# Mixers of a two-layer decoder: splitting the q and k projections by pairs of heads, and the order around it

## The chip, the cores and the metric

One core of one Trainium2 chip runs the whole program in one launch. The metric is the time on the device in microseconds (us), the median of the runs. An execution's time is a little longer than its span in the profile, which goes from the first to the last instruction.

The engines are named as in the profile: PE is TensorE (matmuls; PEld are its weight loads), DVE is VectorE, ACT is ScalarE, POOL is GpSimd, and SP is SyncE, which issues nearly all transfers here. L650 is line 650 of the kernel before.

## What is computed

Two layers on 528 positions (16 meta tokens and 512 of the input) of 1024 features. Each has a mixer and a gated feed-forward part with a short convolution. The mixer is where the change lies:

```python
def mixer_sublayer(h, ...):
    u = rms_norm(h, pre_g)
    z = jnp.einsum("bld,de->ble", u, w_in)
    q, k, v, f_logit, a_val, a_gate, sc_b, sc_c, sc_x = jnp.split(z, idx, axis=-1)
    log_f = jax.nn.log_sigmoid((f_logit + b_forget).astype(jnp.float32))
    y_attn = forgetting_attention(q, k, v, log_f)       # 8 heads of 64
    a = causal_depthwise_conv(a_val * jax.nn.sigmoid(a_gate), a_dw_w) + a_dw_b    # 31 taps
    a = jax.nn.silu(layer_norm(a, a_ln_g, a_ln_b))
    y_conv = jnp.einsum("blc,ce->ble", a, a_pw_w)
    y_sc = sc_b * causal_depthwise_conv(sc_c * sc_x, sc_conv_w)                   # 3 taps
    y = jnp.concatenate([y_attn, y_conv, y_sc], axis=-1)
    y = jnp.einsum("ble,ed->bld", head_rms_norm(y, head_g), w_out)
    return h + rms_norm(y, post_g)

# attention: logit[t,s] = q_t.k_s / 8 + F[t] - F[s] for s <= t, F = inclusive cumsum of log_f
```

## The kernel before

**Layout and arithmetic.** Features lie on the 128 partitions and positions along the free axis, in two halves of 264. Every large product is made of three fp32r matmuls: each operand x is split into a high part (x rounded to fp32r, written by ACT) and a low part (x minus its high part, written by DVE), and high times high, low times high and high times low are added in PSUM. `mm3` at L650 issues these, so L650 stands for all projections, for w_out and for the feed-forward products. Weights come by transfer into `raw`, are split by ACT (`whi`, L619 in planned stretches) and DVE (`wlo`, L623) into rotating buffers, three of the normal kind and five wide ones.

**The order.** In a mixer and in the products that follow it (`finish`), an event simulation at build time (class `Flow`) decides the order of the instructions on each engine. Every operation is given to it with an engine, a planned duration, the tokens it waits for, a priority (a lower number goes first) and a latency; generators called threads stand for PE's work. The resulting order of each engine is fixed in the program. At run time an engine waits only for semaphores, in that order. `flow.run(flow.settled)` ends a planned stretch when what is left has priority 2 or more, which is the default of weight loads and splits (`plan_block`).

**A mixer.** `fill` runs the projections in the order of `mixer_steps()`: q and k blocks hold two heads each (q j and k j are heads 2j and 2j+1), v blocks four heads; sc_b, sc_c and sc_x belong to the short convolution; "pw" starts `conv_tail`, the layer norm, SiLU and pointwise product of the 31-tap convolution. The taps themselves (L966, 60 instructions a layer) are DVE's filler with priority 4. Side by side with `fill` run:

- `maxima`: for each head, PE makes the logits from the high parts of q and k alone (L1372), DVE takes each row's maximum (L1379), POOL puts the negated maxima on a diagonal (L1387), a matmul with ones turns them into a row (L1396), and ACT copies the row into a spare partition of the q tile (L1398). A head's maxima start when the head before has begun its logits.
- `exponentials`: `logits` (two matmuls, L1416: the second one brings the products with the low parts), ACT's exponential (L1423) into tile `pf`, POOL's clearing of the causal corner (L1430), and `weigh` (L1450), the product with v into one accumulator bank (`acc`, a single bank). Each head has two query ranges, 0 to 128 and 128 to 528. After each, ACT evacuates the bank twice, Square into `sq` (L1463) and copy into `yta` (L1464); both must be done before the bank is used again.
- `att_norms`: for each pair of heads a matmul over `sq` (L1516; its tokens are `norm_mm`), then the head norm on ACT and DVE, whose last results are `yhi` and `ylo` (L1123, L1124; their tokens are `norm_at`).
- `Early`: the first two blocks of w_out, accumulated block by block as the eight blocks of y become ready, once `fill` and `maxima` are over.

**Tiles of q and k.** For head hd, `kh[hd % 4]` and `qh[hd % 4]` hold two tiles of 128 partitions each. The head's own 64 rows (`main`) lie at 0 or at 64, the other 64 (`other`) hold the bias rows of the first tile and the low or repeated high part in the second. Tile 1 of q has the high part in `main`; tile 2 has the low part in `other` and the high part again in `main`. Tile 1 of k has the high part in `main`; tile 2 the low part in `main` and the high part again in `other`. In `q_proj` and `k_proj` each half of a block is split head by head, on 64 partitions, straight out of PSUM into place (ACT L1298 and L1326, DVE L1303 and L1331), and a transfer makes the second copy of the high part (`dma`, issued at L530). Tokens: `q_at` and `k_at` release the maxima, `q2_at` the logits. `q_proj(j)` for j of 2 and 3 begins when the logits of the heads four before are done, because the tiles are used again. The gate's rows of k are written by transfers of one row (`gate_rows`).

**After the mixer.** `finish` does the other six blocks of w_out. Block m=3 takes a rotating weight buffer which the early products hold until their end.

Of the kernel before, what the change touches and what calls it, by code (L numbers as in the profile page):

```python
# [9 lines left out]
F32 = mybir.dt.float32  # L10
# [39 lines left out]
NP = 6  # L50

# [169 lines left out]
class Flow:  # L221
# [136 lines left out]
def tile_hybrid_trunk(ctx: ExitStack, tc: tile.TileContext, xT, wflat, pv_d, out):  # L358
# [170 lines left out]
    def dma(out, in_, *after, **kw):  # L529
        return flow.op("sp", 0.35, lambda: nc.sync.dma_start(out, in_), after, **kw)  # L530
# [75 lines left out]
    def plan_block(i, prio):  # L606
# [21 lines left out]
        a = act(act_us(sz), high, got, prio=prio, takes=[(ring, b.slot)])  # L628
# [309 lines left out]
    def mixer(l, ypool, first, close_first, spans, front=None, rz0=None):  # L938
# [351 lines left out]
        def q_proj(j):  # L1290
# [4 lines left out]

            def high(hd, c, ps):
                main = rows(hd)[0]
                nc.scalar.activation(qh[hd % 4][0][main, c], ps[main], AF.Copy, scale=DH ** -0.5)  # L1298

            def low(hd, c, ps):  # L1300
                main, other, _ = rows(hd)
                q1, q2 = qh[hd % 4]
                nc.vector.scalar_tensor_tensor(q2[other, c], in0=ps[main], scalar=DH ** -0.5,  # L1303
                                               in1=q1[main, c].bitcast(F32), op0=ALU.mult, op1=ALU.subtract)

            def use(hf, ps, tok):
                out = []
                for hd in (2 * j, 2 * j + 1):
                    c = half_sl(hf)
                    a = act(act_us(H), lambda hd=hd: high(hd, c, ps), tok, prio=0)  # L1310
                    d = dve(dve_us(H), lambda hd=hd: low(hd, c, ps), a, prio=0)
                    q_at.setdefault(hd, [zeros[hd]] if hd in zeros else []).append(a)
                    q2_at.setdefault(hd, []).append(d)
# [3 lines left out]
            yield from proj(use)  # L1317
            for hd in (2 * j, 2 * j + 1):
                main = rows(hd)[0]
                q1, q2 = qh[hd % 4]  # L1320
                q2_at[hd].append(dma(q2[main].bitcast(F32), q1[main].bitcast(F32), *q_at[hd], lat=2.2))
# [724 lines left out]
```

## Time and profile before

| | |
|---|---|
| runs | 1314.52, 1310.79, 1311.38 us, median 1311.38 |
| profiled execution | 1311.54 us, span 1309.8 us |
| first mixer | about 25 to 225 us of the span |
| second mixer | about 678 to 885 us |
| mean granted TensorE clock | 0.996 |

In the groups of instructions a row is: line, engine, operation, tile written <- tiles read, shapes, count, then busy time in us, mean ns of one, then idle time of the engine before them and what ended it. In lists of waits the three numbers are the total in us, how many, and the longest. In rows in order of time the first two numbers are start and duration in us; square brackets hold the idle time before. Tile names are without buffer numbers: `psum` is all of PSUM.

### The profile page before, as it was taken

What the parts mean: (1) busy time and instruction counts of PE and PEld (TensorE: products, weight loads), DVE (VectorE), ACT (ScalarE), POOL (GpSimd) and SP (SyncE); (2) the same over time, 40 slices, a digit from 0 to 9 for tenths busy, and PEclk for the clock granted to TensorE, in tenths of its full rate; (3) what the DMA queues carried; (4) which work ended last, traced back from release to release, by engine and by line L of the source; (5) the groups of instructions that cost most, each with busy time, mean ns of one, the idle gap of its engine ahead of it and who ended that gap; (6) DMA issues with size and microseconds to landing.
All of it is one profiled execution on the core that took longest, in us unless ns stands there. A gap on an engine that the chain in (4) does not pass through costs nothing. (4 is left out here: it accounts for less than half of the span.)

```text
span 1309.8 us, 23934 instructions
## 1 busy us (share of the span) xinstructions
PE 1282.9 (98%) x9802; PEld 1228.0 (94%) x9802; DVE 865.1 (66%) x1473; ACT 621.2 (47%) x1167; POOL 97.7 (7%) x254
## 2 busy tenths in 40 slices
PE   8999999999999999999989999999999999999997
PEld 8989898999999999999989898889999799989997
DVE  7888865688634663566676888656876246646664
ACT  7255567564423342344662556675643233314353
POOL 1322311000000000000003223110000000000000
PEclk9999999999999999999989999999999999999999
DMA  6133111602222223223340332125032233233321
GB/s 236 34 99 89 60 58 50 223 20 85 94 95 83 98 72 106 91 85 99 108 137 18 99 90 71 47 74 200 17 97 97 85 94 95 71 110 96 92 71 65
DMA packets 42797, 118.26 MB, mean 90 GB/s; under 512 B 4848, under 2 KB 15216, under 8 KB 42688
## 3 DMA queue, kind: packets, MB, share of 16 engines
q1 hardware_dynamic: 42640, 116.61, 28.0%
q8 instruction: 77, 1.26, 0.4%
q14 instruction: 32, 0.26, 0.1%
q0 software_dynamic: 48, 0.13, 0.0%
HBM read 108.04 MB, written 4.33 MB: 86 GB/s over the span
## 5 line engine op out<-in xcount | busy, mean ns | idle before, releaser
L650 PE MATMUL psum<-uhi,whi 128*128 128x264 f32 (+1 forms) x1936 | 451.5, 287 | 1.9 <-ACT uhi L831 1.1
L650 PE MATMUL psum<-ulo,whi 128*128 128x264 f32 (+1 forms) x1936 | 446.7, 285 | 0.5 <-DVE ulo L1827 0.4
L650 PE MATMUL psum<-uhi,wlo 128*128 128x264 f32 (+1 forms) x1936 | 444.8, 284 | 0.0
L650 PEld LDWEIGHTS psum<-uhi,whi 128*128 128x128 f32 x1936 | 322.9, 189 | 5.8 <-issue 2.4
L650 PEld LDWEIGHTS psum<-ulo,whi 128*128 128x128 f32 x1936 | 323.8, 189 | 1.4 <-DVE ulo L1827 0.6
L650 PEld LDWEIGHTS psum<-uhi,wlo 128*128 128x128 f32 x1936 | 323.7, 189 | 0.0
L650 PE MATMUL psum<-yhi,whi 128*128 128x264 f32 (+3 forms) x888 | 249.6, 304 | 1.5 <-ACT yp L1978 1.0
L650 PE MATMUL psum<-ylo,whi 128*128 128x264 f32 (+3 forms) x888 | 245.6, 299 | 1.0 <-DVE ylo L1124 0.8
L650 PE MATMUL psum<-yhi,wlo 128*128 128x264 f32 (+3 forms) x888 | 245.5, 299 | 1.0 <-DVE wlo L623 0.9
L505 ACT CAST whi<-raw 128x1024 fp32r<-128x1024 f32 (+1 forms) x110 | 113.3, 1031 | 213.0 <-PE psum L650 199.4
L506 DVE TENSOR_TENSOR wlo<-raw,whi 128x1024 fp32r<-128x1024 f32 (+1 forms) x110 | 131.9, 1200 | 81.6 <-ACT whi L505 79.5
L650 PEld LDWEIGHTS psum<-yhi,whi 128*128 128x128 f32 x888 | 159.1, 188 | 10.1 <-ACT yp L1978 1.4
L650 PEld LDWEIGHTS psum<-ylo,whi 128*128 128x128 f32 x888 | 159.3, 188 | 7.6 <-DVE ylo L1124 2.0
L650 PEld LDWEIGHTS psum<-yhi,wlo 128*128 128x128 f32 x888 | 159.1, 188 | 7.2 <-DVE wlo L623 1.8
L1927 DVE SCALAR_TENSOR_TENSOR c<-z,pv,c 128x528 f32<-128x528 f32 (+1 forms) x176 | 132.0, 756 | 2.7
L623 DVE TENSOR_TENSOR wlo<-raw,whi 128x1024 fp32r<-128x1024 f32 (+2 forms) x86 | 102.4, 1205 | 36.6 <-ACT whi L619 35.9
L619 ACT CAST whi<-raw 128x1024 fp32r<-128x1024 f32 (+2 forms) x86 | 87.7, 1033 | 32.4 <-DMA raw<-in_w_dram 17.3
L966 DVE SCALAR_TENSOR_TENSOR cacc<-apad,pv,cacc 128x528 f32<-128x528 f32 x120 | 87.7, 772 | 0.5
L1945 ACT CAST yhi<-c 128x528 fp32r<-128x528 f32 (+1 forms) x44 | 27.6, 627 | 111.3 <-DVE c L1941 111.3
L1937 ACT ACTIVATE c<-c 128x528 f32<-128x528 f32 (+1 forms) x44 | 28.1, 639 | 81.7 <-DVE c L1927 81.7
L1890 DVE TENSOR_TENSOR z<-psum,rz 128x528 f32<-128x528 f32 x40 | 28.3, 708 | 53.8 <-PE psum L650 52.2
L1925 ACT ACTIVATE c<-z,pv 128x528 f32<-128x528 f32 (+1 forms) x88 | 63.3, 726 | 0.0
(212 smaller groups left out, 1438.2 us busy)
## 6 DMA issues: line engine op xcount, KB each, us to landing
raw<-in_w_dram SPq DMA_DIRECT2D x160, 512.0 KB
raw<-in_w_dram SPq DMA_DIRECT2D x32, 448.0 KB
h<-in_x_dram SPq DMA_DIRECT2D x16, 264.0 KB
raw<-in_w_dram SPq DMA_DIRECT2D x4, 528.0 KB
q<-q SPq DMA_DIRECT2D x16, 132.0 KB
k<-k SPq DMA_DIRECT2D x16, 132.0 KB
h_dram<-h SPq DMA_DIRECT2D x4, 528.0 KB
h<-h_dram SPq DMA_DIRECT2D x8, 264.0 KB
```

What stands on the lines that cost most here:

```text
L505: nc.scalar.copy(hi[:, :sz], raw[:, :sz])
L506: nc.vector.tensor_sub(lo[:, :sz], raw[:, :sz], hi[:, :sz].bitcast(F32))
L619: nc.scalar.copy(box["hi"][:, :sz], box["raw"][:, :sz])
L623: nc.vector.tensor_sub(lo[:, :sz], box["raw"][:, :sz], box["hi"][:, :sz].bitcast(F32))
L650: nc.tensor.matmul(d, lhsT=w[a][:, k, cols], rhs=rhs(b, k, hf), start=start and i == 0 and p == 0, stop=stop and i == n - 1 and p == 2)
L966: nc.vector.scalar_tensor_tensor(conv[j], in0=src, in1=conv[j], scalar=col("a_dw_w", CK * j + i), op0=ALU.mult, op1=ALU.add)
L1890: nc.vector.tensor_mul(two(t[:, off:]), srcs[0], two(rz))
L1925: nc.scalar.activation(dst, src[:, 2:2 + 2 * fw], AF.Copy, scale=wtap(2, t))
L1927: nc.vector.scalar_tensor_tensor(dst, in0=src[:, i:i + 2 * fw], scalar=wtap(i, t), in1=dst, op0=ALU.mult, op1=ALU.add)
L1937: silu = nc.scalar.activation(cs[0], cs[0], AF.Silu)
L1945: nc.scalar.copy(ghi, cs[0])
```

## The change

1. Heads 2 to 7: `split_pair` writes both heads' high and low parts with one ACT and one DVE instruction for each half of a block, 128 partitions at once, into two new tiles (`pair_hi`, `pair_lo`, two buffers each). Transfers (`part`) then carry each head's 64 rows to where they belong: three for q (high to tile 1, low and high to tile 2) and three for k. The first logits operand now also comes by transfer.
2. Heads 0 and 1: split head by head as before (`split_heads`); the low part of k is now made by the same kind of instruction as that of q.
3. The plan's durations on SP: 0.6 us for a part, 0.95 for a gate row, 0.4 for other transfers, where all had 0.35; gate rows have a priority just over 1 that grows with the head.
4. The evacuations of the accumulator have priority 0 instead of 1, and the Square waits for `norm_mm` of the pair before, instead of `norm_at` of it.
5. `mixer_steps`: pw comes before k 3 instead of after the second sc_c (the stream of weights follows that order).
6. The split of w_out's block m=3 has priority -0.5 (URGENT) and waits for the split of the block before; a stretch may end with it still open.

```diff
-    return [("sc_c", 0), ("sc_x", 0), ("v", 0), ("q", 0), ("k", 0), ("sc_b", 0), ("q", 1), ("k", 1), ("q", 2),
-            ("k", 2), ("v", 1), ("q", 3), ("k", 3), ("sc_c", 1), ("pw", 0), ("sc_x", 1), ("sc_b", 1)]
+    return [("sc_c", 0), ("sc_x", 0), ("v", 0), ("q", 0), ("k", 0), ("sc_b", 0), ("q", 1),
+            ("k", 1), ("q", 2), ("k", 2), ("v", 1), ("q", 3), ("pw", 0), ("k", 3), ("sc_c", 1), ("sc_x", 1), ("sc_b", 1)]
...
-        return all(t[0] in self.lasting for t in self.threads) and all(o[0] >= 2 for ops in self.pend.values() for o in ops)
+        return all(t[0] in self.lasting for t in self.threads) and all(o[0] >= 2 or o[0] == URGENT for ops in self.pend.values() for o in ops)
...
-        a = act(act_us(sz), high, got, prio=prio, takes=[(ring, b.slot)])
+        after = []
+        if chunks[i][0] == "w_out" and chunks[i][4][0][0] == 3 * P:
+            after, prio = [coming[-1][1].tok], URGENT
+        a = act(act_us(sz), high, got, *after, prio=prio, takes=[(ring, b.slot)])
         b.tok = dve(dve_us(sz), low, a, prio=prio)
...
-                gate_at[hd].append(dma(kh[hd % 4][0][aux + p:aux + p + 1, :].bitcast(F32), src, *after, lat=2.0))
+                gate_at[hd].append(dma(kh[hd % 4][0][aux + p:aux + p + 1, :].bitcast(F32), src, *after, us=ROW_US, prio=1 + 0.01 * hd, lat=2.0))
...
+            if j == 0:
+                yield from proj(split_heads(j, DH ** -0.5, qh, 0, q_at, q2_at))
+                for hd in (0, 1):
+                    main = rows(hd)[0]
+                    q2_at[hd].append(spread(qh[hd][1], main, lambda hd=hd: qh[hd][0], main, q_at[hd]))
+                return
+            yield from proj(split_pair(j, DH ** -0.5, q_pair))
+            for hd in (2 * j, 2 * j + 1):
+                main, other, _ = rows(hd)
+                q1, q2 = qh[hd % 4]
+                q_at[hd] = [part(q_pair[j], "hi", q1, main, main), *([zeros[hd]] if hd in zeros else [])]
+                q2_at[hd] = [part(q_pair[j], "lo", q2, other, main), part(q_pair[j], "hi", q2, main, main)]
+            q_pair[j]["slot"].close()
+
+        q_pair, k_pair, pair_ring = {}, {}, Ring(NPAIR)
+
+        def spread(t, to, source, main, after):
+
+            return flow.op("sp", PART_US, lambda: nc.sync.dma_start(t[to].bitcast(F32), source()[main].bitcast(F32)),
+                           after, lat=2.2)
+
+        def part(box, name, t, to, main):
+
+            tok = spread(t, to, lambda: box[name], main, box[name, "at"])
+            box["slot"].use(tok)
+            return tok
...
+        def split_pair(j, scale, pairs):
+
+            box = pairs[j] = {"slot": Slot(), ("hi", "at"): [], ("lo", "at"): []}
+
+            def use(hf, ps, tok):
+                c = half_sl(hf)
+
+                def high():
+                    if hf == 0:
+                        box["hi"], box["lo"] = (T(ap, [P, L], F32R, f"pair_{n}", NPAIR) for n in ("hi", "lo"))
+                    nc.scalar.activation(box["hi"][:, c], ps, AF.Copy, scale=scale)
+
+                def low():
+                    nc.vector.scalar_tensor_tensor(box["lo"][:, c], in0=ps, scalar=scale, in1=box["hi"][:, c].bitcast(F32),
+                                                   op0=ALU.mult, op1=ALU.subtract)
+
+                a = act(act_us(H), high, tok, *box["hi", "at"], prio=0, takes=() if hf else [(pair_ring, box["slot"])])
+                d = dve(stt_us(H), low, a, prio=0)
...
         def k_proj(j):
...
+            yield from proj(split_pair(j, 1.0, k_pair))
             for hd in (2 * j, 2 * j + 1):
                 main, other, _ = rows(hd)
                 k1, k2 = kh[hd % 4]
-                q2_at[hd].append(dma(k2[other].bitcast(F32), k1[main].bitcast(F32), *k_at[hd], lat=2.2))
+                k_at[hd] = [part(k_pair[j], "hi", k1, main, main)]
+                q2_at[hd] += [k_at[hd][0], part(k_pair[j], "lo", k2, main, main), part(k_pair[j], "hi", k2, other, main)]
                 if j > 1:
                     gate_rows(hd, *g_done)
+            k_pair[j]["slot"].close()
             k2_at[j] = True
...
-                waits = norm_at.get(pr - 1 if e == 0 else None, [zero]) + norm_at.get(pr - 1, [zero])
+                waits = norm_mm.get(pr - 1, [zero])
                 n = qz - qa
-                a = act(act_us(n), lambda: nc.scalar.activation(sq[:, qa:qz], acc[:, :n], AF.Square), tok, *waits)
-                c = act(act_us(n), lambda: nc.scalar.copy(yt[r, qa:qz], acc[r, :n]), tok)
+                a = act(act_us(n), lambda: nc.scalar.activation(sq[:, qa:qz], acc[:, :n], AF.Square), tok, *waits, prio=0)
+                c = act(act_us(n), lambda: nc.scalar.copy(yt[r, qa:qz], acc[r, :n]), tok, prio=0)
                 slot.close(a, c)
```

More of the change, by code (lines that the diff above doesn't have):

```diff
@@ L50 @@
 NP = 6
+URGENT = -0.5
+NPAIR = 2
+PART_US, ROW_US = 0.6, 0.95
 WARM, WARM_US = 44, 8.0
@@ L527, in gp, with dma @@
         return flow.op("pool", us, fn, after, **kw)
-    def dma(out, in_, *after, **kw):
-        return flow.op("sp", 0.35, lambda: nc.sync.dma_start(out, in_), after, **kw)
+    def dma(out, in_, *after, us=0.4, **kw):
+        return flow.op("sp", us, lambda: nc.sync.dma_start(out, in_), after, **kw)
     class Early:
@@ L1348, in k_proj @@
+        def k_proj(j):
+            if j == 0:
+                now = {}
+                yield from proj(split_heads(j, 1.0, kh, 1, now, q2_at))
+                for hd in (0, 1):
+                    main, other, _ = rows(hd)
+                    k_at[hd] = now[hd]
+                    q2_at[hd] += [*now[hd], spread(kh[hd][1], other, lambda hd=hd: kh[hd][0], main, now[hd])]
+                k2_at[0] = True
+                return
+            yield from proj(split_pair(j, 1.0, k_pair))
             for hd in (2 * j, 2 * j + 1):
```

51 lines of the change are left out of this document (15 added, 36 removed).

## The prediction

> **What bounds the kernel now.** I read the first page first: busy time by engine, then the granted clock in forty slices.
>
> ```profile
> span 1309.8 us, 23934 instructions
> PE 1282.9 (98%) x9802; PEld 1228.0 (94%) x9802; DVE 865.1 (66%) x1473; ACT 621.2 (47%) x1167; POOL 97.7 (7%) x254
> PEclk9999999999999999999989999999999999999999
> ```
>
> The matrix engine works 98% of the span at a full clock, and the diff adds and removes no matmul. So the change can win only what the matrix engine now waits, in the two mixers alone. The same execution took 1311.54 us, which is the span plus 1.7 us around it; it is 0.16 us over the median 1311.38, so a sum made against it holds for the median.
>
> Second, busy time by stretch, cut where each mixer's filler work runs out. The columns are the stretch, its length, then PE, weight loads, DVE, ACT and POOL.
>
> ```profile
> 25.00:195.00 170.00, 167.24 (x1268) 155.51 (x1267) 137.12 (x316) 91.50 (x224) 43.00 (x103) 1.00 0.24 71
> 195.00:202.00 7.00, 4.81 (x28) 3.56 (x28) 6.45 (x13) 4.70 (x15) 1.93 (x3) 1.00 0.35 107
> 202.00:225.00 23.00, 22.59 (x157) 19.76 (x156) 12.78 (x32) 18.68 (x55) 1.69 (x9) 1.00 0.04 14
> 678.00:848.00 170.00, 166.82 (x1267) 155.26 (x1267) 127.06 (x292) 88.45 (x219) 43.76 (x105) 1.00 0.21 63
> 848.00:855.00 7.00, 4.82 (x29) 3.56 (x28) 6.59 (x14) 4.96 (x16) 1.95 (x3) 1.00 0.34 92
> 855.00:885.00 30.00, 29.12 (x210) 26.04 (x211) 17.05 (x35) 24.40 (x64) 1.51 (x5) 1.00 0.22 72
> ```
>
> PE idles 2.8 us in the long first part of layer 0's mixer, 2.2 us in seven microseconds at 195, and 0.4 us after; in layer 1, 3.2, 2.2 and 0.9 us. All of it together, 11.6 us (0.9%), is the most that the change could bring. Third, whom PE waits for:
>
> ```profile
> PE psum L1450 <- POOL pf L1430: 4.1, 6, 1.3
> PE psum L1450 <- ACT sq L1463: 1.8, 2, 0.9
> PE psum L1264 <- DVE gt L1256: 1.4, 2, 0.7
> PE psum L650 <- DVE wlo L623: 0.9, 3, 0.4
> PE psum L1222 <- DVE fx L1211: 0.8, 1, 0.8
> PE psum L650 <- DVE ylo L1124: 0.8, 3, 0.3
> ```
>
> The waits for gt and fx belong to the forget gate, which the diff leaves alone. Those for the evacuation's Square (sq), the cleared probabilities (pf), the weights' low part (wlo) and the head norm's low part (ylo) are within its reach. Fourth, the place where two of them meet, in order of time (start, duration, engine, line):
>
> ```profile
> 195.79 0.28 PE L650 MATMUL psum<-uhi,wlo 128*128 128x264 f32 x1
> 196.99 0.94 PE L1450 MATMUL psum<-pf,vals 128*128 128x400 f32 x2 [0.92 <-ACT sq L1463]
> 200.29 0.73 PE L1450 MATMUL psum<-pf,vals 128*128 128x272 f32 x2 [1.27 <-POOL pf L1430]
> ...
> 192.05 0.25 ACT L1464 COPY yta<-psum 64x128 f32<-64x128 f32 x1
> 196.67 0.27 ACT L1463 ACTIVATE sq<-psum 128x128 f32<-128x128 f32 x1
> ...
> 195.22 0.42 DVE L1124 TENSOR_TENSOR ylo<-yta,yhi 128x264 fp32r<-128x264 f32 x1
> ...
> 198.74 1.75 POOL L1430 TENSOR_SCALAR_AFFINE_SELECT pf<-pf 128x128 f32<-128x128 f32 x2 [7.97 <-ACT pf L1423]
> 198.87 1.22 DVE L623 TENSOR_TENSOR wlo<-raw,whi 128x1024 fp32r<-128x1024 f32 x1
> ```
>
> This is head 6. The single accumulator bank needs two evacuations. The copy ran at 192.05, the Square only at 196.67: its wait asks for the end of the previous pair's head norm (norm_at), and that is the ylo which ends at 195.64. The bank stayed shut till 196.94, and meanwhile the filler was used up.
>
> **The change, part by part.** *Evacuation (norm_mm, prio 0).* The Square's tile is read only by the norm's matmuls, and waiting for them is enough. The Square can then run beside the copy or before it, so the bank opens at about 192.3 at the latest, 4.6 us earlier, while filler is still there. PE's lost time is more than the idle column says: starts at 195.79 and 196.99 are 1.20 apart, where undisturbed ones are 0.12 apart (229.06 and 229.18 in the rows on the weights below), so 1.08. The same pair of waits stands in layer 1's stretch from 848 (4.82 busy of 7). Gain 2 x 1.08 = **2.1**, between 0 and 2.2.
>
> *The clear behind it.* The second wait is a chain: bank open late, exponential late, clear at 198.74, and that clear met two VectorE instructions and took 1.5 us instead of 0.3:
>
> ```profile
> L1430 POOL TENSOR_SCALAR_AFFINE_SELECT pf<-pf x32: 282/293/1502, 87.8 to 212.6; 128x128 f32<-128x128 f32 x32
> ```
>
> With everything 4.6 us earlier this meeting does not take place; another may. The six such waits cost 4.1 us over 64 clears of both mixers, 0.06 us for a clear drawn afresh. I take nearly the whole 1.27 off in both layers: 2 x 1.2 = **2.4**, bounds 0 and 2.5. The Trainium skill (SBUF — State Buffer, "Who interferes with whom") says that a VectorE instruction with two SBUF inputs blocks a GpSimd instruction that reads SBUF for its whole length. The trace agrees (1.22 us of L623 beside a clear of 1.5 instead of 0.29), and by that rule nothing which blocks is removed here, so the term could be 0 and the sum 2.4 us smaller; that is the first rival.
>
> *Weights.* w_out's fourth block (m=3) takes a rotating buffer that comes free only with the early products; its split now goes first on ACT and DVE. In layer 0:
>
> ```profile
> 229.06 0.28 PE L650 MATMUL psum<-yhi,whi 128*128 128x264 f32 x1
> 229.18 0.28 PE L650 MATMUL psum<-ylo,whi 128*128 128x264 f32 x1
> 229.66 0.39 PE L650 MATMUL psum<-yhi,wlo 128*128 128x264 f32 x1 [0.19 <-DVE wlo L623]
> ...
> 223.41 0.39 PE L650 MATMUL psum<-yhi,whi 128*128 128x264 f32 x1
> 224.12 0.39 PE L650 MATMUL psum<-ylo,whi 128*128 128x264 f32 x1 [0.32 <-DVE ylo L1124]
> ```
>
> 0.48 between starts instead of 0.12 is 0.36 lost, and two layers make **0.7**. What it passes on ACT and DVE are evacuations of at most 0.7 us with a free pair of banks behind them, so I charge nothing; without that cover it is 0.7. The ylo wait loses 0.71 - 0.12 = 0.59; attention that is 4.6 us ahead can remove it, or the sc part may end last instead: half of 2 x 0.6, **0.6**, bounds 0 and 1.2.
>
> *Splits two at once.* Per mixer there are six q and k blocks of heads 2 to 7. Each had four ACT and four DVE instructions on 64 partitions and has two of each on 128 now (the rows of q; k has the same shape):
>
> ```profile
> L1298 ACT ACTIVATE q<-psum 64x264 fp32r<-64x264 f32 x16 | 6.1, 383 | 3.6 <-PE psum L650 3.4
> L1303 DVE SCALAR_TENSOR_TENSOR q<-psum,q 64x264 fp32r<-64x264 f32 x16 | 6.9, 430 | 1.2 <-ACT q L1298 0.7
> L966 DVE SCALAR_TENSOR_TENSOR cacc<-apad,pv,cacc x60: 746/762/939, 45.3 to 163.5; 128x528 f32<-128x528 f32 x60
> L1539 PE MATMUL psum<-cacc,om_c x8: 383/386/386, 176.2 to 177.8; 128*128 128x264 f32 x8
> ```
>
> That is 12 x 0.38 = 4.6 us of ACT and 12 x 0.43 = 5.2 us of DVE for each mixer, if the doubled partitions cost no more. It lies beside a full PE (167.24 of 170), so it counts as **0**; the convolution's taps, DVE's filler, end up to 5 us sooner. Until now the tail of the convolution began at 176.2, since the pw block came after sc_c, though the taps ended at 164. With pw ahead of k 3 it starts some 10 us earlier, and its matmuls go ahead of k 3. That only moves PE work, again 0.
>
> *Spreading.* Per block, two transfers become six: 24 more for each mixer, and q's and k's high halves, which the row maxima need, now come by transfer. Until now only the second logits operand did, and was due later.
>
> ```profile
> 170.23 1.10 SPq L530 DMA_DIRECT2D k<-k  x2
> 172.54 0.34 PE L1372 MATMUL psum<-k,q 128*16 128x16 f32 x2
> DMA  0000000000000679999399495920000000000009
> ...
> 116.92 1.11 SPq L530 DMA_DIRECT2D q<-q  x2
> DMA  0099565748999577978979631110000000000000
> ```
>
> The first activity row is 170 to 174 us in 40 slices: two transfers issued at 170.23 move from 171.3 to 172.7, so one alone is in place some 1.9 us after its issue (half of that traffic), and six take about 1.2 + 6 x 0.7 = 5.4. The plan reckons 0.6 + 2.2 = 2.8 for one. The second is 116 to 122: two transfers behind a weight load end at 120.9, 4.0 after their issue, 1.2 over plan. Row maxima follow k at once for heads 2 and 6 alone (170.23 and 172.54 above are head 6), so four places in two layers. Loads of the kind take about 0.2 of this time (DMA share 0.24 and 0.21). Bounds 0 and 4 x 1.2 = 4.8; I take 0.2 x 4.8 = **1.0**, nearest to undisturbed transfers. On SP, the weight loads behind these six wait some 6 x 0.55 = 3.3 us; they have a lower priority already and splits are done ahead. The gate rows' new length and order cost SP plan time only. Delay of heads 6 and 7 itself costs nothing while PE has filler: sc_c, sc_x and sc_b of the second half are 3 x 48 x 0.12 = 17 us.
>
> **Sum**: -2.1 - 2.4 - 0.7 - 0.6 + 1.0 = -4.8; 1311.5 - 4.8 = **1306.7 us**, 0.36% under the median. A difference under 0.3% (3.9 us) I count as no change that a measurement of this kernel tells.
>
> **Rivals.**
>
> *The wait moves on.* The clear meets another two-input VectorE instruction, or PE finds itself behind another clear: then only 2.4 is left, 1309.1 us. For it: four of the six waits for pf lie elsewhere already, where the change gives no cause to lessen them. Against it: at 195 to 202 the filler was gone, and it will not be.
>
> *Transfers late (the other side).* The high halves come behind weight loads, and PE, whose order is fixed when the program is made, stands before the maxima. Each of the 12 blocks can cost 1.2 us. The gains are 5.8; slower by 0.3% needs 5.8 + 3.9 = 9.7, so eight late blocks of the 12. With nine, 10.8 - 5.8 = +5.0, 1316.5 us. For it: the plan knows nothing of transfers meeting in the queues, and 4.0 us has been seen. Against it: heads 3, 4, 5 and 7 have several microseconds to spare, since maxima of a head start only when the head before has begun its logits.
>
> *More is won.* The re-planned mixers lose other waits too, half of the remaining 11.6 - 4.8 = 6.8 us: 1303.3 us. For it: relieved ACT and DVE; against it, the first 170 us already idle only 1.6 to 1.9%.
>
> **How the numbers follow.** Forecast 0.42 (its own range 1305 to 1308.5), wait moves on 0.28, transfers late 0.17, more won 0.13. The time is that of the forecast. The bound of "faster" is 1307.4: 0.33 of the forecast's 0.42 lies below, and with 0.13 that makes 0.46; the rest 0.09 + 0.28 = 0.37 is no change; 0.17 slower. The range 1303 to 1313.5 leaves out most of the late transfers (0.15) and a little of the best case.
>
> **What would show it.** Right: no wait of L1450 for sq; Square and copy of one head next to each other; PE's busy share from 195 to 202 near 7 of 7; ACT and DVE with 24 instructions fewer each; the convolution's mean matmuls before 170 us. Wrong: a new wait of PE at the maxima (L1372) for a transfer of q or k; long clears before L1450 elsewhere; or the early products of w_out standing for y of the short convolution at the mixer's end, because the tail has been emptied of other work.

## The result, and the profile after

The median went from 1311.09 to 1301.74 us (four runs each, 1310.42 to 1314.52 and 1301.25 to 1302.07). The ratio is 0.9923 with a 95% interval of 0.9905 to 0.9941: some 9.4 us faster, twice the 4.8 us of the forecast and 1.3 us under the low end of its range.

The first page of the changed kernel. In this kernel the lines have moved: what was L650 is L656, L1372 is L1414, L1396 and L1398 are L1438 and L1440, L1430 is L1472, L1450 is L1492, L1463 and L1464 are L1505 and L1506, L1136 is L1142, L1539 is L1581; the transfers of the pairs are issued at L1320, the gate's rows at L533.

```profile
span 1300.2 us, 23941 instructions
PE 1278.3 (98%) x9802; PEld 1226.7 (94%) x9802; DVE 852.7 (66%) x1449; ACT 612.2 (47%) x1143; POOL 96.2 (7%) x254
```

The matrix engine has the same 9802 matmuls and 24 instructions fewer stand on each of DVE and ACT. The span is 9.6 us shorter, but PE's idle time (span less busy) fell only from 26.9 to 21.9 us. The other 4.6 us came off its busy time, 1282.9 to 1278.3, for the same matmuls. A matmul that follows a wait is booked longer (0.39 instead of 0.28 us in the prediction's rows on the weights and in rows below), so part of each wait had been counted as work. The granted clock is not the reason: it is at one half for one spell of 6.8 us in each of the two executions, ahead of layer 1's mixer, which is the 8 in the prediction's row PEclk. The weight loads show more of it: span less PEld was 81.8 us and is 73.5, 8.3 less.

Busy time by stretch, the columns as in the prediction; layer 0's three stretches, then layer 1's, each shorter mixer cut at its own end.

```profile
25.00:195.00 170.00, 166.61 (x1257) 154.42 (x1256) 134.07 (x313) 92.63 (x229) 41.94 (x102) 1.00 0.32 89
195.00:202.00 7.00, 7.00 (x50) 6.15 (x49) 5.91 (x14) 5.12 (x16) 1.65 (x4) 1.00 0.24 77
202.00:221.00 19.00, 19.00 (x144) 17.42 (x143) 10.36 (x24) 12.31 (x33) 2.60 (x9) 1.00 0.09 28
674.00:844.00 170.00, 167.94 (x1269) 156.10 (x1268) 127.46 (x293) 91.24 (x231) 42.89 (x106) 1.00 0.30 81
844.00:851.00 7.00, 7.00 (x58) 6.83 (x57) 5.08 (x12) 4.43 (x12) 0.90 (x3) 1.00 0.24 73
851.00:874.00 23.00, 23.00 (x181) 21.41 (x181) 11.08 (x21) 16.35 (x42) 2.36 (x5) 1.00 0.36 109
```

In the seven microseconds at 195, PE now starts 50 matmuls where it started 28, and in layer 1's 58 where it started 29. From 195 to the end there is no idle time left. The first 170 us of layer 0 idle a little more than before (3.4 against 2.8 us), those of layer 1 less (2.1 against 3.2).

What PE waits for in the mixers and just behind them (total, times, longest, in us):

```profile
PE psum L1261 <- DVE fpre L1256: 1.7, 2, 0.9
...
PE psum L1438 <- POOL dm L1429: 0.9, 2, 0.4
...
PE psum L1142 <- ACT q L1440: 0.8, 2, 0.4
PE psum L656 <- DVE wlo L626: 0.7, 2, 0.4
PE psum L1492 <- POOL pf L1472: 0.6, 2, 0.3
PE psum L656 <- ACT uhi L885: 0.5, 1, 0.5
...
PE psum L656 <- DVE ulo L887: 0.3, 1, 0.3
```

The waits for sq and ylo are gone, those for pf went from 4.1 to 0.6 us, the two for wlo lie at 9.4 and 13.0 us, before the first mixer, and none is for a transfer. Those for dm and q (steps of the row maxima) are new, 1.7 us together. The forget gate's own waits changed too, though the diff leaves it alone: gt, fx and fpre had 3.0 us, fpre alone has 1.7 now. The wait for uhi and ulo stands behind the mixer and is new; it is taken up below.

Head 6 in order of time, in the layer and at the place that the prediction showed:

```profile
194.90 0.38 PE L1492 MATMUL psum<-pf,vals 128*128 128x128 f32 x2
195.31 0.28 ACT L1505 ACTIVATE sq<-psum 128x128 f32<-128x128 f32 x1 [0.45 <-PE psum L1492]
195.49 0.25 ACT L1506 COPY yta<-psum 64x128 f32<-64x128 f32 x1
196.21 0.83 PE L1492 MATMUL psum<-pf,vals 128*128 128x400 f32 x2
196.26 0.83 POOL L1472 TENSOR_SCALAR_AFFINE_SELECT pf<-pf 128x128 f32<-128x128 f32 x1 [2.87 <-ACT pf L1465]
```

Square and copy follow the matmuls at once, where 4.6 us lay between them, and the bank is written again at 196.21, 1.3 us after the start of the products that filled it.

Groups of the tiles that the change touches, in layer 0's mixer: durations in ns (shortest, median, longest), then the start of the first and of the last.

```profile
L1363 ACT ACTIVATE pair_hi<-psum x12: 368/391/393, 91.3 to 174.0; 128x264 fp32r<-128x264 f32 x12
L1366 DVE SCALAR_TENSOR_TENSOR pair_lo<-psum,pair_hi x12: 427/432/433, 92.4 to 174.4; 128x264 fp32r<-128x264 f32 x12
L1320 SPq DMA_DIRECT2D q<-pair_hi x12: 461/588/594, 98.8 to 165.9; - x12
DMA to landing us min/median/max: 2.2/2.3/2.4
...
L1472 POOL TENSOR_SCALAR_AFFINE_SELECT pf<-pf x32: 292/293/1289, 88.6 to 211.7; 128x128 f32<-128x128 f32 x32
...
L1581 PE MATMUL psum<-cacc,om_c x8: 385/386/386, 163.6 to 165.2; 128*128 128x264 f32 x8
L1142 PE MATMUL psum<-apad,bd x8: 383/386/461, 183.1 to 188.3; 128*128 128x264 f32 x8
L1492 PE MATMUL psum<-pf,vals x20: 271/415/603, 194.9 to 212.9; 128*128 128x400 f32 x8, 128*128 128x128 f32 x4, 128*128 128x272 f32 x4, 128*128 128x144 f32 x4
```

A split on 128 partitions takes what one on 64 took (0.39 and 0.43 us). The convolution's mean is 12.6 us earlier than before. The last two rows are the two tails of the mixer: the head norm of the convolution's output (apad), and the products of heads 6 and 7 with v. Before, they were:

```profile
L1136 PE MATMUL psum<-apad,bd x8: 383/386/386, 210.2 to 215.9; 128*128 128x264 f32 x8
L1450 PE MATMUL psum<-pf,vals x20: 270/416/603, 189.1 to 213.4; 128*128 128x400 f32 x8, 128*128 128x128 f32 x4, 128*128 128x272 f32 x4, 128*128 128x144 f32 x4
```

Attention ends almost where it did (212.9 against 213.4), while the convolution's tail is through 27.6 us earlier, at a time when there is still other work for PE.

Where in the program the time fell is told by pairing the n-th matmul of one trace with the n-th of the other (start after less start before, us). The orders differ inside a mixer, so only the rows behind a mixer are exact.

| matmul number | where | difference |
|---|---|---|
| 1300 | inside layer 0's mixer | +0.9 |
| 1800 | layer 0's mixer over | -4.6 |
| 5300 | before layer 1's mixer | -4.5 |
| 6800 | layer 1's mixer over | -11.8 |
| 7500 and the last | feed-forward part of layer 1, end | -9.7 |

Layer 0 brings 4.6 us, layer 1 another 7.2, and 2.1 of it is given back at once, in the first products of layer 1's feed-forward part. These wait for their input, the residual sum's normalised halves:

```profile
920.99 0.39 PE L656 MATMUL psum<-uhi,whi 128*128 128x264 f32 x1 [0.52 <-ACT uhi L885]
921.63 0.39 PE L656 MATMUL psum<-ulo,whi 128*128 128x264 f32 x1 [0.25 <-DVE ulo L887]
```

### The profile page after: what moved, and what is told of

Its sections match the earlier page's. It is cut to its first block, busy times and chain, and to the rows that moved or that the text cites. A ratio compares the mean times of both kernels' runs of the same rounds, so it can differ in the third digit from the quotient of the medians.

```text
span 1300.2 us, 23941 instructions
## 1 busy us (share of the span) xinstructions
PE 1278.3 (98%) x9802; PEld 1226.7 (94%) x9802; DVE 852.7 (66%) x1449; ACT 612.2 (47%) x1143; POOL 96.2 (7%) x254
## 5 line engine op out<-in xcount | busy, mean ns | idle before, releaser
L656 PE MATMUL psum<-uhi,whi 128*128 128x264 f32 (+1 forms) x1936 | 454.9, 287 | 2.8 <-ACT uhi L837 1.1
L656 PE MATMUL psum<-ulo,whi 128*128 128x264 f32 (+1 forms) x1936 | 449.2, 285 | 0.8 <-DVE ulo L1869 0.4
L656 PE MATMUL psum<-uhi,wlo 128*128 128x264 f32 (+1 forms) x1936 | 447.3, 284 | 0.0
L656 PEld LDWEIGHTS psum<-uhi,whi 128*128 128x128 f32 x1936 | 324.0, 189 | 8.2 <-issue 1.9
L656 PEld LDWEIGHTS psum<-ulo,whi 128*128 128x128 f32 x1936 | 325.0, 189 | 1.9 <-DVE ulo L1869 0.6
L656 PEld LDWEIGHTS psum<-uhi,wlo 128*128 128x128 f32 x1936 | 324.8, 189 | 0.0
L656 PE MATMUL psum<-yhi,whi 128*128 128x264 f32 (+3 forms) x888 | 247.7, 302 | 1.4 <-ACT yp L2020 1.0
L656 PE MATMUL psum<-yhi,wlo 128*128 128x264 f32 (+3 forms) x888 | 245.4, 299 | 0.7 <-DVE wlo L626 0.7
L656 PE MATMUL psum<-ylo,whi 128*128 128x264 f32 (+3 forms) x888 | 245.0, 298 | 0.0
L656 PEld LDWEIGHTS psum<-yhi,whi 128*128 128x128 f32 x888 | 159.0, 188 | 8.7 <-ACT yp L2020 1.4
L656 PEld LDWEIGHTS psum<-yhi,wlo 128*128 128x128 f32 x888 | 159.1, 188 | 6.4 <-DVE wlo L626 1.1
L656 PEld LDWEIGHTS psum<-ylo,whi 128*128 128x128 f32 x888 | 159.3, 188 | 5.4
L1987 ACT CAST yhi<-c 128x528 fp32r<-128x528 f32 (+1 forms) x44 | 27.6, 627 | 108.6 <-DVE c L1983 108.6
```

Of the source, the lines that this page charges most:

```text
L656: nc.tensor.matmul(d, lhsT=w[a][:, k, cols], rhs=rhs(b, k, hf), start=start and i == 0 and p == 0, stop=stop and i == n - 1 and p == 2)
L1987: nc.scalar.copy(ghi, cs[0])
```

## The experiments

The change has four separable parts: the evacuation (item 4 of the change), the order (5), the pairs with their transfers and SP lengths (1 to 3), and the weights (6). A kernel without the pairs splits all eight heads as item 2 splits the first two. The kernels without the pairs also have the gate rows' old length and priority on SP, and all kernels made from the changed one plan DVE's splits at 0.49 us where the kernel before has 0.44. The expectations call the theories by names of their own; each is told before the runs that it belongs to. Ratios are to the kernel before in the same batch. Differences in us to the whole change are between medians of different batches, in which the kernel before stood at 1311.1 to 1312.9 us, so they are good to one or two us.

**First: each part alone, and each taken out.** Theory at this point: the Square's wait and what hung on it brought most. Rival: the order did, because the convolution's tail no longer ends last. The evacuation alone:

```diff
-                waits = norm_at.get(pr - 1 if e == 0 else None, [zero]) + norm_at.get(pr - 1, [zero])
+                waits = norm_mm.get(pr - 1, [zero])
...
-                a = act(act_us(n), lambda: nc.scalar.activation(sq[:, qa:qz], acc[:, :n], AF.Square), tok, *waits)
-                c = act(act_us(n), lambda: nc.scalar.copy(yt[r, qa:qz], acc[r, :n]), tok)
+                a = act(act_us(n), lambda: nc.scalar.activation(sq[:, qa:qz], acc[:, :n], AF.Square), tok, *waits, prio=0)
+                c = act(act_us(n), lambda: nc.scalar.copy(yt[r, qa:qz], acc[r, :n]), tok, prio=0)
```

> The kernel before with the evacuation's new wait (norm_mm) and priority alone; heads are split one by one, in the old order. Theory 1 (the late Square is the main cause): the waits of L1450 for sq and for pf near the end of each mixer go, and most of the gain is here: 1311.1 - 5 to 7 = 1304 to 1306 us. Theory 2 (the order decides: pw ahead of k 3 takes the convolution's tail out of the mixer's end): the Square's wait goes but the tail stays crowded: 1308.5 to 1310.5. Theory 3 (relief of ACT and DVE by the pair splits decides): the same 1308.5 to 1310.5.

Measured: 1315.69 us, ratio 1.0019 (1.0009 to 1.0029): 0.2% slower, which is no more than a newly drawn plan does (fourth batch). The two tails in its trace:

```profile
L1142 PE MATMUL psum<-apad,bd x8: 383/385/386, 216.7 to 221.2; 128*128 128x264 f32 x8
L1496 PE MATMUL psum<-pf,vals x20: 272/392/501, 189.8 to 202.4; 128*128 128x400 f32 x8, 128*128 128x128 f32 x4, 128*128 128x272 f32 x4, 128*128 128x144 f32 x4
```

The part does what it says: attention is over at 202.4, eleven microseconds earlier. But the convolution's tail, which ran beside it, now comes last, and later (221.2 against 215.9). The whole kernel with the old evacuation (the same lines the other way round):

> The changed kernel with the old wait (norm_at) and old priority of the evacuations. Theory 1: the Square is late again and most of the gain is lost: 1306 to 1309 us. Theories 2 and 3: 1302 to 1304, as the other parts keep their gain.

Measured: 1317.08, ratio 1.0033 (1.0022 to 1.0045): 15 us over the whole change. What PE waits for there:

```profile
PE psum L656 <- DVE rs_t L1111: 4.1, 4, 1.8
PE psum L1438 <- DVE rs_t L1111: 4.1, 2, 2.1
```

L1111 is the head norm's step that reads its sums out of PSUM. PE stands before a bank that this step still holds, and attention ends at 221.1. Not all of the 15 us is waiting. Behind two such waits (2.05 and 1.83 us) the matmuls of 264 columns start 0.22 us apart instead of 0.12, and the granted clock reads 0.50 from 204 to 210 us:

```profile
204.71 0.59 PE L656 MATMUL psum<-uhi,whi 128*128 128x264 f32 x1 [1.83 <-DVE rs_t L1111]
205.10 0.42 PE L656 MATMUL psum<-ulo,whi 128*128 128x264 f32 x1
205.32 0.42 PE L656 MATMUL psum<-uhi,wlo 128*128 128x264 f32 x1
```

The clock is taken up after the fifth batch. The order alone:

```diff
-            ("k", 2), ("v", 1), ("q", 3), ("k", 3), ("sc_c", 1), ("pw", 0), ("sc_x", 1), ("sc_b", 1)]
+            ("k", 1), ("q", 2), ("k", 2), ("v", 1), ("q", 3), ("pw", 0), ("k", 3), ("sc_c", 1), ("sc_x", 1), ("sc_b", 1)]
```

> The kernel before with pw ahead of k 3 alone. Theory 2: the convolution's mean matmuls begin near 164 us instead of 176, the tail of the mixer has fewer ACT and DVE instructions, 1304 to 1307 us. Theories 1 and 3: the Square still waits for the head norm; 1309 to 1312.

Measured: 1312.35, ratio 0.9998 (0.9989 to 1.0006), the same. The convolution's mean comes at 164.2, as with the whole change, but its pointwise products still start at 200.1 to 206.3 (203.5 to 208.1 before): an early mean alone doesn't bring the tail forward. The whole kernel with the old order:

> The changed kernel with the old order of projections (pw after the second sc_c). Theory 2: 1305 to 1309 us. Theories 1 and 3: 1301.5 to 1304.

Measured: 1314.47, ratio 1.0013 (1.0003 to 1.0022): 12.7 us over the whole change.

```profile
L1142 PE MATMUL psum<-apad,bd x8: 386/386/387, 216.6 to 221.0; 128*128 128x264 f32 x8
L1492 PE MATMUL psum<-pf,vals x20: 270/392/499, 189.6 to 204.1; 128*128 128x400 f32 x8, 128*128 128x128 f32 x4, 128*128 128x272 f32 x4, 128*128 128x144 f32 x4
```

The picture of the evacuation alone: attention is over at 204.1, and the convolution's norm at 221 is last. Neither theory holds: neither part alone gains, and with either taken out nothing of the gain is left.

**Second: the pairs, two parts together, the weights.** Theory now: the parts need each other, since each alone only moves the end from one tail to the other. Rival: evacuation and order make the gain between them, and the pairs are neutral. The pairs alone (old evacuation, order and weights):

> The kernel before with the splits two at once, their transfers and the plan's longer SP durations, nothing else. Theory 3 (ACT and DVE relieved): 1304 to 1308 us. Theories 1 and 2: relief lies beside a full PE and transfers cost up to 2 us: 1310.5 to 1313.

Measured: 1320.85, ratio 1.0067 (1.0054 to 1.0079), the slowest of all. Its longest wait in total:

```profile
PE psum L1492 <- ACT yta L1506: 3.9, 3, 2.0
```

The accumulator's copy, still at its old priority and beside the old wait, now costs 3.9 us. The whole kernel without the pairs:

```diff
-            if j == 0:
+            if True:
...
-                for hd in (0, 1):
+                for hd in (2 * j, 2 * j + 1):
...
-PART_US, ROW_US = 0.6, 0.95
+PART_US, ROW_US = 0.35, 0.35
```

> The changed kernel with every head split by itself straight from PSUM and the old SP durations. Theory 3: 1305 to 1309 us. Theories 1 and 2: 1300.5 to 1303, as the transfers' delay goes too.

(The gate rows' priority is the old one too.) Measured: 1312.46, ratio 0.9998 (0.9989 to 1.0007), the same as before the change. Evacuation and order together, without pairs and weights:

> The kernel before with the evacuation's wait and priority and with pw ahead of k 3, no pairs, no urgent split. If the two parts explain the gain between them: 1301.5 to 1303.5 us. If the pairs matter (theory 3): 1304 or more.

Measured: 1311.26, ratio 0.9993 (0.9984 to 1.0002), the same. Here is a wait that the pairs take away. The place is the split of k 3, in order of time:

```profile
170.34 0.28 PE L656 MATMUL psum<-uhi,wlo 128*128 128x264 f32 x1
170.66 0.80 ACT L1335 ACTIVATE k<-psum 64x264 fp32r<-64x264 f32 x2 [0.64 <-PE psum L656]
171.48 0.87 DVE L1340 SCALAR_TENSOR_TENSOR k<-psum,k 64x264 fp32r<-64x264 f32 x2 [0.56 <-ACT k L1335]
172.41 0.39 PE L656 MATMUL psum<-uhi,whi 128*128 128x264 f32 x1 [1.79 <-DVE k L1340]
```

Four short instructions hold one PSUM bank from the matmul's end until 172.35, some 1.7 us, and PE needs that bank next. Two instructions on 128 partitions are 0.39 + 0.43 = 0.82 us. PE's waits for the splits of k and q are 3.6 + 1.9 = 5.5 us over both layers here, the same without the pairs, and none with the whole change. Last, the whole kernel without the urgent weight split:

```diff
-            after, prio = [coming[-1][1].tok], URGENT
+            pass
```

> The changed kernel with w_out's block m=3 split at the old priority. By the prediction's term the wait for wlo comes back, 0.36 us a layer: 1302.2 to 1302.8 us. If the urgent split is what gives back about 2 us in the second layer's first feed-forward products (waits for uhi and ulo near 921 us): 1299.5 to 1301.

Measured: 1303.45, ratio 0.9933 (0.9921 to 0.9946): 1.7 us over the whole change, a difference which the fourth batch shows to be within what a newly drawn plan does.

These runs together, as the ratio to the kernel before:

| evacuation | order | pairs | ratio |
|---|---|---|---|
| yes | | | 1.0019 |
| | yes | | 0.9998 |
| | | yes | 1.0067 |
| yes | yes | | 0.9993 |
| yes | | yes | 1.0013 (with weights) |
| | yes | yes | 1.0033 (with weights) |
| yes | yes | yes | 0.9933; 0.9923 with weights |

No single part and no pair of parts is faster by 0.3%; the three together are. Each row but the last is one plan. The rows without pairs have the old lengths and row priority on SP, which the third and fifth batches show to matter; evacuation and order with the new ones, but without the split by pairs, was not run.

**Third: what it is in each part.** Theory: with the pairs it is the shorter hold of the bank. Rivals: the transfers that bring the high halves, or the lengths on SP. Splits of the pairs in halves of 64 partitions, with tiles and transfers as they are:

```diff
-                    nc.scalar.activation(box["hi"][:, c], ps, AF.Copy, scale=scale)
+                    r = slice(DH * e, DH * (e + 1))
+                    nc.scalar.activation(box["hi"][r, c], ps[r], AF.Copy, scale=scale)
...
+                a2 = act(act_us(H), lambda: high_of(1), tok, a, prio=0)
+                d2 = dve(stt_us(H), lambda: low_of(1), a2, prio=0)
```

> The changed kernel, but each half of a q or k block is split with two ACT and two DVE instructions on 64 partitions each, into the same pair tiles, with the same transfers after. Theory 4 (bank theory: a projection's PSUM bank is held for four short instructions in a chain instead of two, 1.7 us instead of 0.85, and PE waits for that bank when two of the three are held by norms): waits of PE for the split's DVE instruction come back, as the 0.9 and 1.8 us seen without pairs, and the time is 1305 to 1309 us. Theory 5 (what helps is that the tiles of q and k are filled by transfers, off the engines' order): 1301 to 1303.

Measured: 1310.23, ratio 0.9987 (0.9979 to 0.9996), 8.5 us over the whole change. The bank of k 3 is late again:

```profile
169.06 0.42 DVE L1371 SCALAR_TENSOR_TENSOR pair_lo<-psum,pair_hi 64x264 fp32r<-64x264 f32 x1 [0.56 <-ACT pair_hi L1367]
169.53 0.43 DVE L1592 TENSOR_TENSOR cacc<-cacc,psum 128x264 f32<-128x264 f32 x1
169.99 0.43 DVE L1371 SCALAR_TENSOR_TENSOR pair_lo<-psum,pair_hi 64x264 fp32r<-64x264 f32 x1
170.48 1.16 PE L1617 MATMUL psum<-apad,om_c 128*128 128x264 f32 x4 [0.99 <-DVE pair_lo L1371]
```

So with the same transfers and the same numbers on SP, the split by pairs is worth this much. PE's waits for these splits explain 2.8 of it (two waits, one in each layer). Halves also bring back 24 instructions each on ACT and DVE, in the same edit, so the run doesn't tell the bank's hold apart from the load of these engines. The lengths and the gate rows' priority as before:

```diff
-PART_US, ROW_US = 0.6, 0.95
+PART_US, ROW_US = 0.35, 0.35
...
-    def dma(out, in_, *after, us=0.4, **kw):
+    def dma(out, in_, *after, us=0.35, **kw):
...
-... *after, us=ROW_US, prio=1 + 0.01 * hd, lat=2.0))
+... *after, us=ROW_US, lat=2.0))
```

> The changed kernel with the old SP durations in the plan (0.35 for all) and the old priority of the gate rows. If the lengths matter: PE finds itself before row maxima or logits whose transfers are later than planned, 1304 to 1308 us. If the real transfers have enough slack anyway: 1301 to 1303.

Measured: 1315.83, ratio 1.0026 (1.0015 to 1.0036): 14 us lost by numbers in the plan, with the same instructions. No wait of PE names a transfer there. And the two halves of the evacuation, the new wait with the old priority, then the old wait with the new priority:

> The changed kernel with the evacuation's new wait (norm_mm) but the old priority 1. If the wait is what made the Square late: 1301.5 to 1304 us. If the priority matters too (copy and Square behind the convolution's instructions on ACT): 1305 to 1309.

> The changed kernel with the evacuation's new priority 0 but the old wait (norm_at of the pair before). If the wait is what made the Square late: 1306 to 1314 us, like the kernel without both (1317). If the priority alone does it: 1301.5 to 1304.

Measured: 1306.95 (0.9958, 0.9945 to 0.9971) and 1317.31 (1.0039, 1.0026 to 1.0052). Without the new wait the priority is worth nothing; with it, it brings 5.2 us more, just over what a new draw does.

**Fourth: how much is the draw of the plan?** Any edit makes the simulation decide anew, and some of these differences could be luck. Both kernels were drawn again with one number changed that nothing of the change depends on, the planner's time for one engine's signal to reach another:

```diff
-    HOP = 0.06
+    HOP = 0.07
```

and the same with 0.05.

> The changed kernel with the plan's hop between engines at 0.07 us instead of 0.06; nothing else. Theory 6 (the draw of the plan decides several us): 1304 to 1310 us. If the parts decide: 1301 to 1303.

> The changed kernel with the hop at 0.05 us. Theory 6: anywhere from 1302 to 1310, and not near the run with 0.07. If the parts decide: 1301 to 1303.

> The kernel before with the hop at 0.07 us. Theory 6: 1312 to 1320 us, or lower than before by some us. If the parts decide: 1310.5 to 1312.5.

> The kernel before with the hop at 0.05 us. Theory 6: as with 0.07, several us off. If the parts decide: 1310.5 to 1312.5.

Measured: 1302.02 (0.9924, 0.991 to 0.9939), 1304.62 (0.9944, 0.9927 to 0.996), 1313.22 (1.001, 1.0001 to 1.0019) and 1315.34 (1.0028, 1.0016 to 1.004). A new draw moves the time by 0 to 4 us, and the two kernels stay 9 to 11 us apart in each. The gain isn't a lucky draw. The variants in between were drawn once each, so what one of them loses is known to some 4 us; a difference of under 4 us between two variants, that of the weights among them, can't be put down to their edit.

**Fifth: which of the SP numbers.** Theory: the gate rows' priority keeps them from standing ahead of q's parts. Rival: the parts' own length places their users right.

```diff
-PART_US, ROW_US = 0.6, 0.95
+PART_US, ROW_US = 0.35, 0.95
```

> The changed kernel with the parts' duration in the plan at 0.35 us instead of 0.6; gate rows as changed. If the parts' length decides (six in a row are planned 1.5 us shorter than they take, so heads 2, 4 and 6 are placed too early): 1308 to 1316 us. If the gate rows decide: 1301 to 1305.

```diff
-PART_US, ROW_US = 0.6, 0.95
+PART_US, ROW_US = 0.6, 0.35
...
-... *after, us=ROW_US, prio=1 + 0.01 * hd, lat=2.0))
+... *after, us=ROW_US, lat=2.0))
```

> The changed kernel with the gate rows' duration in the plan at 0.35 us and their old priority; parts as changed. If the parts' length decides: 1301 to 1305 us. If the gate rows decide (eight rows at the start shift the whole attention against the projections): 1308 to 1316.

Measured: 1300.76 (0.9909, 0.9896 to 0.9921) with short parts, the fastest median of all and no different from the whole change by the measure of the fourth batch; 1314.68 (1.0015, 1.0006 to 1.0023) with short rows. The parts' length doesn't matter; the rows' length and priority together are the 13 us (they were not separated). How the numbers act is open. The rows stand on SP like this with short rows, in order of time, with ACT's instruction that writes the second half of q 1's high part:

```profile
95.14 8.67 SPq L533 DMA_DIRECT2D k<-g_dram  x4
103.80 0.39 ACT L1363 ACTIVATE pair_hi<-psum 128x264 fp32r<-128x264 f32 x1 [0.28 <-PE psum L656]
104.22 2.40 SPq L1320 DMA_DIRECT2D q<-pair_hi  x4
```

and with the whole change:

```profile
98.43 0.39 ACT L1363 ACTIVATE pair_hi<-psum 128x264 fp32r<-128x264 f32 x1 [0.65 <-PE psum L656]
98.84 2.42 SPq L1320 DMA_DIRECT2D q<-pair_hi  x4
```

With short rows four gate rows stand in a line ahead of q 1's parts, and the last two go out only at 103.3; with the whole change these two go out behind the parts, at 104.0. That looks like a queue whose head holds up the parts, since they start 5.4 us later. But for these parts the traces rule it out: in both plans the parts start 0.02 to 0.03 us after ACT has written what they carry (104.19 and 98.82). In the plan with short rows PE does the second half of q 1's projection itself 5.4 us later, and there the parts had nothing to go for earlier. Layer 1 shows the same (ACT's write ends at 759.11, the parts start at 759.13). As far as these rows show, the numbers act through the order that the plan gives to PE's work, not through the queue. No wait of PE is for a transfer. The longest that the whole change doesn't have come at the mixer's end, for cleared probabilities (2.9 us) and for rows of maxima (1.8 us):

```profile
PE psum L1492 <- POOL pf L1472: 2.9, 4, 1.0
...
PE psum L1458 <- ACT q L1440: 1.8, 2, 0.9
```

**The clock in these runs.** A second cause runs through the losses of the variants. Neither the kernel before nor the whole change has a spell of half clock inside a mixer. The old evacuation has two of 6.8 us (at 204 and 859); old lengths, short rows and the kernel without pairs have two of 3.4 us each, the evacuation alone and the new priority with the old wait one of 3.4. Each begins within some 1.5 us of a wait of PE. While it lasts PE loses at most half its time, so up to 6.8, 3.4 and 1.7 us of these profiled executions' losses are the clock and not the waiting itself; from the spans, what is left over the whole change is still 7 to 12 us. Over all executions of the kernel before, too, the time goes with the mean granted clock: about 1310.8 us at 0.999, 1314.5 at 0.994. That a wait brings the spell on isn't shown by a run: after the same wait of 1.79 us the kernel without pairs has one, evacuation and order together has none.

**What stays open.** Why the three parts are worth nothing until all are there isn't settled by a run that isolates it. Over the plans, one number goes with the time: the start of the last norm product of the convolution's tail in layer 0 (the apad row).

| plans | last apad product at, us | time, us |
|---|---|---|
| whole change, its two new draws, short parts, without weights | 187.7 to 188.3 | 1300.8 to 1304.6 |
| new wait with old priority | 195.8 | 1307.0 |
| old evacuation; old wait with new priority | 195.9; 201.8 | 1317.1; 1317.3 |
| evacuation and order; without pairs; pairs in halves | 199.9; 201.3; 201.5 | 1311.3; 1312.5; 1310.2 |
| old lengths; short rows | 199.4; 199.7 | 1315.8; 1314.7 |
| order alone; before and its new draws; pairs alone | 213.8; 215.9, 219.9, 217.4; 216.1 | 1312.4; 1311.1, 1313.2, 1315.3; 1320.9 |
| old order; evacuation alone | 221.0; 221.2 | 1314.5; 1315.7 |

Only where this tail is through by 188, six to seven us ahead of the last two heads' products with v (194.9 in the whole change), does the time fall under 1305. In the rest it comes close to attention's last heads or runs beside them, where both need ACT, DVE and PSUM banks, and the time then doesn't follow its place. That the meeting is the cause is read from these traces, not shown by a run, and why layer 1 has the larger share (7.2 of 11.8 us) isn't known.

## Why the prediction was right and wrong

**Right.** PE's waits for sq, pf, wlo and ylo were named and 6.3 of their 7.6 us went. That idle time fell by 5.0 us, where the sum said 4.8, is in part luck: 1.3 us less wait of the forget gate is in it, which the prediction left out, and 2.5 us of new waits (dm, q, uhi, ulo) stand against it. By the lists of waits, sq went from 1.8 to 0 and pf from 4.1 to 0.6 us, where the terms said 2.1 and 2.4. The transfers' +1.0 is 0, since no wait for one appears. Doubled partitions cost nothing on ACT and DVE. The five marks of a right forecast were all seen: Square next to copy, no wait for sq, PE at 7.00 of 7 in the stretch at 195, 24 instructions fewer on ACT and DVE, the convolution's mean before 170.

**Where it failed.** The time was outside the range because of these steps:

1. "All of it together, 11.6 us (0.9%), is the most that the change could bring." The gain of 9.4 us stays under it, but layer 1 alone gained 7.2 us where its part of the 11.6 was 6.3 and its idle time fell by 4.2. The column was the wrong measure, and the rest of the prediction was sized by it. The prediction itself found that starts 1.20 us apart hide more than the column says and sized three terms by starts, but its largest, the clear's 2.4, by idle time. In the two seven-microsecond stretches PE started 22 and 29 matmuls more; at 0.12 us each, the spacing of 264-column products there, that is up to 6.1 us, where the idle column held 4.4. Over the whole program as much again as the idle time came off "busy" time (4.6 beside 5.0).
2. "It lies beside a full PE (167.24 of 170), so it counts as 0", of the pair splits. With the same transfers and halves instead of pairs the kernel is 8.5 us slower. One thing that the 0 left out is how long a bank stays shut behind a projection, 1.7 us against some 0.8; without the pairs PE waits 5.5 us for such banks. PE's full share in the kernel before doesn't show it. How much of the 8.5 is the bank and how much ACT's and DVE's time wasn't separated.
3. "That only moves PE work, again 0", of pw ahead of k 3. With the old order the kernel is 12.7 us slower. The mean came forward as predicted (12.6 us), but the pointwise products behind it start at 179 with the whole change, 208 with the old order and 203 in the kernel before, so the move takes them away from attention's last heads. Alone it doesn't (200).
4. "The gate rows' new length and order cost SP plan time only." With the old ones the kernel is 13 us slower, up to 3.4 of it by the clock. The rows above don't show SP's queue to be the way. What they show is another order of PE's work in the plan, and which part of that order costs the time is open.
5. The sum added parts as though each had its worth alone. The evacuation's 2.1 + 2.4 was worked out in a mixer that has the other parts; alone it gains nothing (1.0019), and in its trace attention ends 11 us earlier while the convolution's tail ends later.

The rival "more is won" (1303.3, half of what idles) came nearest and had 0.13; its reason, relieved ACT and DVE, is near to what the halves showed. "The wait moves on" fell: of layer 0's 32 clears twelve take 0.5 to 1.3 us instead of 0.29 (eight took over 0.5 before), each beside an instruction of DVE with two SBUF inputs, as the page of the Trainium skill cited in the prediction says (SBUF — State Buffer, "Who interferes with whom"), but PE now has other work beside them and waits 0.6 us in all. "Transfers late" fell too: the high halves land 2.2 to 2.4 us after their issue, and the 4.0 us that spoke for it didn't come back for them (a low half took 3.8 at most).

## What to carry to other kernels

Where a build-time plan keeps the main engine full, price a change by what ends last and by how long each bank is held, not by the idle column: it showed 5.0 us of a gain of 9.4. When two chains end a stage side by side, shortening one hands the end to the other, so try the parts together before dropping one that brings nothing alone, and draw both plans anew to learn what luck is worth (here 4 us). A transfer that starts late need not have been held up: compare its start with the end of the instruction that writes what it carries. And look at the granted clock of each variant before its loss is put down to waits.

## What the runs showed of the hardware

- The profile counts part of a wait as work: the first matmul after one is booked at 0.39 instead of 0.28 us, and 4.6 us of "busy" went away without a matmul less. The idle time of the weight loads (-8.3 us) came nearer to the gain.
- The granted clock can fall to one half inside a mixer, for 3.4 or 6.8 us in these traces, and 264-column matmuls then start 0.22 instead of 0.12 us apart. Such a spell stood close behind waits of PE, but not behind every one.
- ACT and DVE take the same time for 64 and for 128 partitions of 264 elements (0.39 and 0.43 us).
- Twenty-four more transfers a mixer, of 64 rows each, take 0.59 us of SP apiece and land 2.2 to 2.4 us after issue (high halves of q); with the DMA share up from 0.24 to 0.32 in the long stretch, PE had no wait for one.
